# First stage of a hybrid attention / DeltaNet layer: a fixed table of single instructions in place of a list scheduler

## The chip, the cores and the metric

One core of one Trainium2 chip runs the kernel. The metric is the device time of one execution in microseconds, as the median of several runs. The profiled execution is a separate one, and its views give times within that execution's span.

## What is computed

One decoder layer over 512 tokens of width 1024, in fp32. The layer has two token mixers that read the same combined projection of x, a merge of the two, and an MLP:

```python
q, ck, cv, sk, sv, wk, wv, gates, qkv, beta, decay, gg, mg = split(x @ w_in)
o_nsa = g0 * compressed_attn + g1 * selected_block_attn + g2 * window_attn      # 8 heads of 64, 2 key groups
o_gdn = rms_norm(gated_deltanet(conv(qkv), beta, decay)) * silu(gg)              # 4 heads of 128, 4 chunks here
m = sigmoid(mg[:1024]) * (o_nsa @ w_nsa_out) + sigmoid(mg[1024:]) * (o_gdn @ w_gdn_out)
x = LN(alpha * x + m @ w_o)
x = LN(alpha * x + (silu(conv(x @ w_up)[gate]) * conv(x @ w_up)[val]) @ w_down)
```

## The kernel before

Every fp32 product is made of three f32r products of a high and a low half: `product` (L234) issues, for each of eight 128-row blocks, hi·hi (L239), hi·lo (L241) and lo·hi (L242), so that one weight unit of 128 output columns is 24 matmuls of 512 columns. `gemm_t` (L247) is such a unit: `split_w` (L215) loads 512 KB of weights into `raw` (DMA, L218), copies each half to f32r as `wh` (L225 on ACT, or L227 on DVE), subtracts for the rest `wl` (L229, DVE or POOL), and the product goes to a PSUM bank of the pool `pg` that has two.

The first stage (L261 to L882) begins with x: `load_x` (L209) loads and splits it, and `pb` products of 288 columns (L276 to L278) give the values and gate inputs token by token. Then come the small constants (L297 to L316), the decay terms `decays` (L331 to L367, whose prefix sums are the small matmuls L365), and steps named by a letter and a head. For GDN head h: `i` (`gdn_k`), `j` (`gdn_q`), `v` (`gdn_v`), `m` (`gdn_mid`: decay matrices and the kq products L482), `n` (`gdn_tri`: inverse of the triangular matrix, whose first block sums are L495, L497, L503 and the matmuls L505, and then 15 steps of two small DVE operations, L512 and L513), `o` (`gdn_out`: the four chunks in turn), `y` (`gdn_gate`: norm with the power L258 on POOL, transposes L397 of `y`, gating multiply L631 to `yT`). For attention: `k` keys, `q` queries of two heads, `c` the compressed blocks (L694 among others), `p` the compressed attention of a key group, `a` and `b` the six score units of a head, of which each goes through scores (L781, L782), a fused mask and maximum (L785), exp (L787), a scale (L798), transposes (L810), a split copy (L814, L815) and PV matmuls (L827, L832) into the one `pout` bank. `oT` (L838) takes a head's result. `g` is a merge product (`merge`, L855): a weight unit whose tanh goes to an SBUF tile `mt` (L858).

What sets the order before is a list scheduler. The step list `ORDER` (L128) gives each step a priority from its place, moved by `SHIFT` (L125); the weight splits are moved by `PRE` (L127); the scheduler then places the instructions of every engine one by one, taking what its own model holds ready by priority. Work tiles come out of pools with rotating buffers, a tag for each kind of use (`BUFS`, L129).

The merge stage follows (L884 to L928): `yoh` (copies L146 and L148 of `oT` and `yT`) and `yol` (L905), then for m from 0 to 7 a pair of `pm` products against `w_nsa_out` and `w_gdn_out`, each the size of half a unit, the gating, and the load and split of `w_o`. Five merge products are done in the first stage (`g0` to `g4`), two more ahead of m = 0, the rest between the pm products, in a PSUM pool `pg2` of their own:

```python
done = BUFS["mg"]
for m in range(8):
    while done < min(16, max(2 * m + 4, BUFS["mg"] + 2)):
        merge(done, mg2)
        done += 1
```

## Time and profile before

| | |
|---|---|
| time, 3 runs | median 842.46 us (842.21 to 843.61) |
| profiled execution | 845.36 us, of which span 843.6 us, mean granted clock 0.995 |
| TensorE busy | 822.8 us (98%) |
| VectorE, ScalarE, GpSimd busy | 637.8 (76%), 407.5 (48%), 145.4 us (17%) |
| chain that ended last | PE 80%, DVE 10%, ACT 3%, issue 3%, DMA 3% |
| first stage until the first pm matmul | 0 to 349.1 us |
| merge stage, output product, MLP | 349 to 843.6 us |

A matmul's recorded duration is longer than the distance to the next one, since they are pipelined. So a busy TensorE is not one at its rate: for the rate, the starts of successive matmuls are compared.

### The profile page before, as it was taken

Reading aid. Unit: us, or ns where it says so; the run is one execution under the profiler, and the core shown is the slowest. Engines: PE = TensorE matmul, PEld = TensorE weight load, DVE = VectorE, ACT = ScalarE, POOL = GpSimd, SP = SyncE. Lnnn points to the kernel's source line nnn. Section 1 sums busy time; section 2 is a strip of 40 time slices with the busy share of each in tenths; the row PEclk is TensorE's granted clock in tenths of the full one; section 3 lists DMA queues with packets and bytes.
Section 4 is the critical chain, followed back from the end, with each engine's and each line's share of the span. In section 5 each row is a group of like instructions: output and inputs, shape, how many; then the busy total and the mean of one; then the engine's idle time right before and its main releaser. Section 6 shows DMA issues by size and latency. Waiting matters only on the chain.

```text
span 843.6 us, 12073 instructions
## 1 busy us (share of the span) xinstructions
PE 822.8 (98%) x4226; PEld 679.7 (81%) x4226; DVE 637.8 (76%) x1373; ACT 407.5 (48%) x916; POOL 145.4 (17%) x127
## 2 busy tenths in 40 slices
PE   9899999999999999999999999999999999999996
PEld 8787787878777778888888898888888888788884
DVE  5856789987856985863457637888888988998578
ACT  5343577575457755442234114444444444566350
POOL 0131222313243321201400002101111111100001
PEclk9999999999999999999999999999999999999998
DMA  7323120002111101254346021555555566665762
GB/s 249 128 76 100 51 76 26 26 27 75 51 32 44 51 26 50 93 167 141 124 133 244 25 76 51 199 200 200 198 188 192 197 199 202 223 223 189 262 205 107
DMA packets 39820, 108.06 MB, mean 128 GB/s; under 512 B 4560, under 2 KB 4944, under 8 KB 39504
## 3 DMA queue, kind: packets, MB, share of 16 engines
q1 hardware_dynamic: 39760, 107.30, 38.5%
q8 instruction: 33, 0.54, 0.3%
q14 instruction: 27, 0.22, 0.1%
HBM read 93.65 MB, written 13.63 MB: 127 GB/s over the span
## 4 chain that ended last, share of the span: by engine, by line
PE 80%; DVE 10%; ACT 3%; issue 3%; DMA 3%; POOL 1%; SPq 0%; DVEq 0%; ACTq 0%; POOLq 0%
PE pu L241 9%; PE pu L239 9%; PE pu L242 9%; PE gps L241 7%; PE gps L239 7%; PE gps L242 7%; PE pout L827 2%; PE pw L988 2%; PE pw L989 2%; PE pw L990 2%; PE pm L242 2%; PE pm L239 2%; PE pm L241 2%; PE aps L810 2%; PE pdnb L1123 1%
## 5 line engine op out<-in xcount | busy, mean ns | idle before, releaser
L225 ACT ACTIVATE wh<-raw 128x512 fp32r<-128x512 f32 (+1 forms) x162 | 100.2, 621 | 122.7 <-PE pu L241 68.0
L239 PE MATMUL pu<-mh,wh 128*128 128x512 f32 (+1 forms) x384 | 142.7, 372 | 0.0
L241 PE MATMUL pu<-ml,wh 128*128 128x512 f32 (+1 forms) x384 | 142.6, 371 | 0.0
L242 PE MATMUL pu<-mh,wl 128*128 128x512 f32 (+1 forms) x384 | 142.6, 371 | 0.0
L229 DVE TENSOR_TENSOR wl<-raw,wh 128x512 fp32r<-128x512 f32 (+1 forms) x144 | 113.9, 793 | 34.7 <-ACT wh L225 33.2
L239 PE MATMUL gps<-xh,wh 128*128 128x512 f32 x320 | 128.5, 402 | 0.6 <-DVE kl L648 0.6
L241 PE MATMUL gps<-xl,wh 128*128 128x512 f32 x320 | 128.2, 401 | 0.0
L242 PE MATMUL gps<-xh,wl 128*128 128x512 f32 x320 | 127.8, 400 | 0.0
L239 PEld LDWEIGHTS pu<-mh,wh 128*128 128x128 f32 x384 | 72.3, 188 | 12.6
L242 PEld LDWEIGHTS pu<-mh,wl 128*128 128x128 f32 x384 | 72.3, 188 | 12.6
L241 PEld LDWEIGHTS pu<-ml,wh 128*128 128x128 f32 x384 | 72.3, 188 | 12.3
L229 POOL TENSOR_TENSOR wl<-raw,wh 128x512 fp32r<-128x512 f32 x40 | 53.7, 1343 | 153.0 <-ACT wh L225 81.0
L1067 DVE SCALAR_TENSOR_TENSOR fa<-pu,fcw,fa 128x511 f32<-128x511 f32 x88 | 65.7, 746 | 9.3 <-ACT fa L1064 7.9
L239 PEld LDWEIGHTS gps<-xh,wh 128*128 128x128 f32 x320 | 60.6, 189 | 11.6 <-issue 1.0
L242 PEld LDWEIGHTS gps<-xh,wl 128*128 128x128 f32 x320 | 60.7, 190 | 10.8
L241 PEld LDWEIGHTS gps<-xl,wh 128*128 128x128 f32 x320 | 60.7, 190 | 10.6
L1073 POOL TENSOR_TENSOR fth<-fth,fa 128x512 f32<-128x512 f32 x22 | 29.5, 1339 | 214.1 <-DVE fa L1067 199.9
L1114 DVE TENSOR_TENSOR dl<-raw,dh 128x512 fp32r<-128x512 f32 x69 | 46.0, 703 | 19.4 <-ACT dh L1113 19.2
L1113 ACT ACTIVATE dh<-raw 128x512 fp32r<-128x512 f32 x69 | 41.0, 626 | 36.5 <-DMA raw<-tdn 17.7
L787 ACT ACTIVATE sc<-sc,mn 128x384 f32<-128x384 f32 (+2 forms) x64 | 35.9, 562 | 16.2 <-DVE mn L785 11.7
L258 POOL TENSOR_TENSOR rs<-rs,minus_half 128x1 f32<-128x1 f32 x8 | 7.5, 941 | 163.3 <-DVE rs L949 163.3
L1064 ACT ACTIVATE fa<-pu,fcw 128x512 f32<-128x512 f32 x44 | 29.6, 672 | 10.2 <-PE pu L242 10.2
(350 smaller groups left out, 1688.8 us busy)
## 6 DMA issues: line engine op xcount, KB each, us to landing
raw<-in_up SPq DMA_DIRECT2D x44, 512.0 KB, 4.0
raw<-in_wT SPq DMA_DIRECT2D x40, 512.0 KB, 3.5
traw<-in_down SPq DMA_DIRECT2D x22, 512.0 KB, 4.8
tdn<-traw SPq DMA_DIRECT2D x44, 256.0 KB, 3.3
raw<-tdn SPq DMA_DIRECT2D x20, 512.0 KB, 4.4
raw<-in_down SPq DMA_DIRECT2D x15, 512.0 KB, 3.7
raw<-in_wm SPq DMA_DIRECT2D x8, 512.0 KB, 3.6
raw<-in_wo SPq DMA_DIRECT2D x8, 512.0 KB, 3.9
```

What stands on the lines that cost most here:

```text
L225: A.activation(wh, r, AF.Copy)
L229: eng.tensor_tensor(wl, r, wh.bitcast(F32), op=OP.subtract)
L239: i = PE.matmul(ps, wh[k], mh_(k), start=(k == 0), stop=False)
L241: PE.matmul(ps, wh[k], ml_(k), start=False, stop=False)
L242: PE.matmul(ps, wl[k], mh_(k), start=False, stop=(k == n - 1))
L787: A.activation(s[:, i, :n], s[:, i, :n], AF.Exp, scale=-1.0, bias=mn[:, 0, i:i + 1], accum_out=mn[:, 1, i:i + 1])
L810: PE.transpose(pt[:, i, k, :], s[:, i, k * 128:(k + 1) * 128], ident)
L1064: A.activation(acc, ps, AF.Copy, scale=w[:, 2:3])
L1067: V.scalar_tensor_tensor(acc[:, n:], ps[:, :S - n], w[:, i:i + 1], acc[:, n:], op0=OP.mult, op1=OP.add)
L1073: G.tensor_tensor(th, th, g[1], op=OP.mult)
L1113: A.activation(wh, raw[:, i], AF.Copy)
L1114: V.tensor_tensor(wl, raw[:, i], wh.bitcast(F32), op=OP.subtract)
```

## The change

Engine calls of the first stage are no longer issued where they are written. A `Queue` around each engine records them under the name of their step (`draw`), and a table `GIVEN` of 2,822 single instructions then gives them out one after the other, with no scheduler between (`tc.manual_schedule()`). An entry such as `q0P*12` stands for the next twelve TensorE instructions of step q0, `dV@2` for a certain one of the decays on DVE; weight units have steps of their own (`w20S`, `w20A`, `w20V`), so their load and split stand apart from the product; `s` and `f` with two digits are the score and the PV part of a unit. P has 1,610 entries, V 688, A 415, G 74, S 35. The instructions after the first stage are written and scheduled as before.

Work tiles of the stage come from `Places`: a fixed set of tiles of each size, of which a string names the one that each request gets. In place of ten tags there are ten sizes, shared between uses.

Seven merge products stand in the table. The sixth and seventh stay in the two `pg` banks, which are kept open past the stage, and `gate` (their tanh) is written behind the loop that makes `yoh` and `yol`. The merge stage asks for nine merge products ahead of m = 0, and takes its PSUM banks from the same `pg`.

```diff
-ORDER = "q0 k0 i0 q1 j0 m0 c n0 ...
-SHIFT = {'q0': -40, 'a0': -3470, ...
-PRE = {17: 2170, 13: -300, ...
+DRAWN = "q0 k0 i0 q1 j0 m0 c n0 ... g3 a7 g4 b7 y3 g5 g6".split()
+GIVEN = """
+w20S w20A w20V w20A w20V n0V@2 q0P*12 w18S dV@2 dV@3 dA@1 w0S q0P*10 dV@4 dV@5 dV@6 w18A n2G@1 w18A w18V dV@7 w18V
...
+y3V y3P*4 y3V f75A f75V g6P
+""".split()
+    class Queue:
+        def __getattr__(self, name):
+            give = getattr(self.engine, name)
+            def note(*a, **kw):
+                if not into:
+                    return give(*a, **kw)
+                steps[into[-1]].setdefault(self.letter, []).append((give, a, kw))
+            return note
...
+    class Places:
+        def tile(self, shape=(128, S), dt=F32):
+            t = self.all[next(self.turn)][:shape[0], :math.prod(shape[1:])]
...
-        acc = slot("in", "acc")
+        acc = R["big"].tile()
...
     def merge(i, pl):
-        ps = gemm_t(24 + i)
+        MG[i] = gemm_t(24 + i)
+        if pl is not None:
+            gate(i, pl)
+
+    def gate(i, pl):
         t = pl.tile([128, S], F32, name="mt", bufs=BUFS["mg" if pl is mgp else "mr"])
-        A.activation(t, ps, AF.Tanh, scale=0.5)
+        A.activation(t, MG[i], AF.Tanh, scale=0.5)
         MG[i] = t
...
-    for step in ORDER:
-        with tc.high_priority(offset=-(at + SHIFT.get(step, 0))):
-            f(*[int(step[1:])] if step[1:] else [])
...
+    with tc.manual_schedule():
+        for step in GIVEN:
+            name, at, k = step.partition("@")
+            name, _, n = name.partition("*")
+            for _ in range(int(n or 1)):
+                part = todo[name]
+                i = int(k) if at else next(i for i, x in enumerate(part) if x)
+                give, a, kw = part[i]
+                part[i] = None
+                give(*a, **kw)
...
     pm = ps2.enter_context(tc.tile_pool(name="pm", bufs=2, space=PSUM))
-    pg = ps2.enter_context(tc.tile_pool(name="pg2", bufs=2, space=PSUM))
-    gps = lambda shape=(128, 512): pg.tile(list(shape), F32, name="gps")
...
     done = BUFS["mg"]
+    while done in MG:
+        gate(done, mg2)
+        done += 1
     for m in range(8):
-        while done < min(16, max(2 * m + 4, BUFS["mg"] + 2)):
+        while done < min(16, max(2 * m + 4, BUFS["mg"] + 4)):
             merge(done, mg2)
             done += 1
```

Three places of the two orders follow. In the names of the changed kernel `pg_171` and `pg_172` are the two banks of `pg`, `po_398` is the `pout` bank, `pd` and `pa` are other PSUM tiles, and `big` and `row` are work tiles; L252 and L1023 are the lines from which all its recorded or given calls are issued.

SyncE's queue at the start, before (from the last but one block of `wB` on):

```order
8 L218 DMA raw<-in_wB 128x576
9 L218 DMA raw<-in_wT 128x1024
10 L211 DMA xr<-in_xT 128x512
11 L297 DMA cst<-in_consts 128x1444
12 L300 DMA ident<-in_consts 128x128
13 L307 DMA gcw<-in_gcw 128x48
14 L309 DMA fcw<-in_fcw 128x132
```

And now (from the last block of `wB` on):

```order
11 L252 DMA raw_156<-in_wB 128x576
12 L252 DMA big_94<-in_xT 128x512
13 L252 DMA cst<-in_consts 128x1444
14 L252 DMA ident<-in_consts 128x128
15 L252 DMA gcw<-in_gcw 128x48
16 L252 DMA fcw<-in_fcw 128x132
17 L252 DMA gnw<-in_gnw 128x1
18 L252 DMA alog<-in_glog 128x4
19 L252 DMA gdt<-in_gdt 128x4
20 L1023 DMA raw_157<-in_wT 128x1024
```

The first weight unit (`in_wT`) stood ahead of the last load of x; now it stands behind it and behind the seven loads of constants.

TensorE at the first block sums of GDN head 0, before: the last two kq products (L482), what lies between, and the block sums (L505):

```order
290 L482 MATMUL dps<-kq 128x256
291 L694 MATMUL aps<-kv,raw 128x155 x3
292 L241 MATMUL gps<-xl,wh 128x512
293 L242 MATMUL gps<-xh,wl 128x512
294 L239 MATMUL gps<-xh,wh 128x512
295 L241 MATMUL gps<-xl,wh 128x512
296 L242 MATMUL gps<-xh,wl 128x512
297 L239 MATMUL gps<-xh,wh 128x512
298 L241 MATMUL gps<-xl,wh 128x512
299 L242 MATMUL gps<-xh,wl 128x512
300 L505 MATMUL dps<-gx,cst 128x512
```

And now (`pd_394<-kq` is the last kq product, `pd_393<-big_87,cst` the first block sum):

```order
260 L1023 MATMUL pg_171<-xl,wh_160 128x512
261 L1023 MATMUL pd_394<-kq_117 128x256
262 L1023 MATMUL pg_172<-xh,wh_161 128x512
263 L1023 MATMUL pg_172<-xl,wh_161 128x512
...
278 L1023 MATMUL pg_172<-xh,wl_162 128x512
279 L1023 MATMUL pg_172<-xh,wh_159 128x512
280 L1023 MATMUL pg_172<-xl,wh_159 128x512
281 L1023 MATMUL pg_172<-xh,wl_162 128x512
282 L1023 MATMUL pg_172<-xh,wh_159 128x512
283 L1023 MATMUL pd_393<-big_87,cst 128x512
```

Between the last kq product and the first block sum there were three matmuls of 155 columns and eight of 512; there are now 21 of 512 (rows 262 to 282).

ACT at the end of the first stage, before:

```order
374 L146 ACTIVATE ob<-pout 64x512
375 L611 ACTIVATE gt<-gps 128x512
376 L146 ACTIVATE yoh<-oT 128x512 x2
377 L146 ACTIVATE yoh<-yT 128x512 x4
378 L858 ACTIVATE mt<-gps 128x512
```

And now:

```order
386 L252 ACTIVATE wh_159<-raw_157 128x512
387 L1023 ACTIVATE big_109<-po_398 64x512
388 L252 ACTIVATE yoh<-oT 128x512 x2
389 L252 ACTIVATE yoh<-yT 128x512 x4
390 L252 ACTIVATE mt<-pg_172 128x512
391 L252 ACTIVATE mt<-pg_171 128x512
```

TensorE there, now (`pd_393<-ident,big_101` are the transposes of `y` of GDN head 3; `pg_171` and `pg_172` are the banks in which the seventh and the sixth merge product lie):

```order
1423 L1023 MATMUL po_398<-pc_154,vcb 128x512
1424 L1023 MATMUL po_398<-pc_155,vcb 128x512
1425 L1023 MATMUL pd_393<-ident,big_101 128x128 x4
1426 L1023 MATMUL pg_171<-xh,wl_164 128x512
1427 L252 MATMUL pg_172<-xh,wh_161 128x512
1428 L252 MATMUL pg_172<-xl,wh_161 128x512
```

The tanh that reads a merge product stood behind the six `yoh` copies before and stands behind them now. Before, TensorE wrote the next product into another bank than the one which that tanh reads; now the next one (row 1427) goes into `pg_172`, which the first of the two tanh reads.

## Rows read from the trace of the kernel before

**Rows 1.** The page's first, second and sixth section: busy time of the engines in the whole span, the granted clock in 40 equal slices, and the loads of the weight units (KB each, median us from issue to landing).

```profile
PE 822.8 (98%) x4226; PEld 679.7 (81%) x4226; DVE 637.8 (76%) x1373; ACT 407.5 (48%) x916; POOL 145.4 (17%) x127
...
PEclk9999999999999999999999999999999999999998
...
raw<-in_wT SPq DMA_DIRECT2D x40, 512.0 KB, 3.5
```

**Rows 2.** Busy time of each engine in stretches of the program (length, then PE, PEld, DVE, ACT, POOL busy with the count of instructions, granted clock, DMA share, GB/s): one stretch inside the first stage, the last two merge products, and the merge stage from its first pm matmul on.

```profile
140.00:180.00 40.00, 38.16 (x247) 30.21 (x245) 36.73 (x116) 23.70 (x58) 11.87 (x10) 1.00 0.14 41
341.00:349.00 8.00, 8.00 (x37) 6.61 (x36) 5.93 (x11) 5.71 (x10) 2.92 (x2) 1.00 0.21 68
349.00:442.00 93.00, 93.00 (x412) 77.02 (x411) 51.02 (x66) 31.23 (x48) 18.84 (x15) 1.00 0.43 142
```

**Rows 3.** TensorE's instructions between the first matmul of q0 and the first pm matmul, grouped by line, operands and shape (count; busy, mean ns; idle time in front of them): the six costliest of 45 groups.

```profile
L239 PE MATMUL gps<-xh,wh 128*128 128x512 f32 x248 | 100.5, 405 | 0.6 <-DVE kl L648 0.6
L241 PE MATMUL gps<-xl,wh 128*128 128x512 f32 x248 | 100.2, 404 | 0.0
L242 PE MATMUL gps<-xh,wl 128*128 128x512 f32 x248 | 99.8, 403 | 0.0
L810 PE MATMUL aps<-ident,sc 128*128 128x128 f32 x160 | 28.1, 276 | 1.1 <-DVE sc L798 1.0
L827 PE MATMUL pout<-pth,vcat 128*128 128x256 f32 x96 | 26.9, 304 | 1.1 <-DVE oT L838 1.0
L827 PE MATMUL pout<-ptl,vcat 128*128 128x256 f32 x96 | 25.0, 291 | 0.2 <-DVE ptl L815 0.2
...
```

**Rows 4.** TensorE's timeline at three places (start, duration, line, operands, count): a PV matmul of 256 columns and the one five starts later; four transposes and the matmul behind them; and two pm matmuls of 512 columns, six starts apart. The distance from start to start is the rate.

```profile
335.64 0.27 PE L827 MATMUL pout<-pth,vcat 128*128 128x256 f32 x1
...
336.23 0.28 PE L827 MATMUL pout<-ptl,vcat 128*128 128x256 f32 x1
...
339.99 0.66 PE L397 MATMUL dps<-ident,y 128*128 128x128 f32 x4
340.40 0.47 PE L241 MATMUL gps<-xl,wh 128*128 128x512 f32 x1
...
349.13 0.39 PE L239 MATMUL pm<-yoh,wh 128*128 128x512 f32 x1
...
350.49 0.39 PE L239 MATMUL pm<-yoh,wh 128*128 128x512 f32 x1
```

**Rows 5.** TensorE's waits in the first stage, by what was waited for (total us, times, longest): the two largest of 13 entries, and the smallest.

```profile
PE dps L365 <- issue: 1.7, 1, 1.7
PE dps L505 <- DVE gx L503: 1.6, 2, 1.2
...
PE pout L827 <- DVE ptl L815: 0.2, 1, 0.2
```

**Rows 6.** SyncE's timeline in the start: the first weight unit's load, the last load of x, the last small load, and the second weight unit's load.

```profile
11.13 0.33 SPq L218 DMA_DIRECT2D raw<-in_wT  x1
11.51 0.42 SPq L211 DMA_DIRECT2D xr<-in_xT  x1
...
16.33 0.33 SPq L316 DMA_DIRECT2D gdt<-in_gdt  x1
17.18 0.33 SPq L218 DMA_DIRECT2D raw<-in_wT  x1
```

**Rows 7.** The load issued at 17.18 us (KB, us from issue to landing).

```profile
raw<-in_wT SPq DMA_DIRECT2D x1, 512.0 KB, 4.6
```

**Rows 8.** TensorE's timeline at the start of q0: the first product matmul.

```profile
19.98 0.39 PE L239 MATMUL gps<-xh,wh 128*128 128x512 f32 x1
```

**Rows 9.** TensorE's timeline around the decay matmuls (L365): they themselves with the idle time in front, and the first and last of nine products that start from 32.20 to 35.55 us.

```profile
30.51 0.81 PE L365 MATMUL dps<-gdec,cst 128*128 128x16 f32 x6 [1.73 <-issue]
...
32.20 0.57 PE L239 MATMUL gps<-xh,wh 128*128 128x512 f32 x1
...
35.55 0.45 PE L242 MATMUL gps<-xh,wl 128*128 128x512 f32 x1
```

**Rows 10.** Busy time and granted clock (the column behind POOL) just after that wait, and after a wait of 1.18 us elsewhere.

```profile
33.00:35.00 2.00, 2.00 (x6) 1.63 (x5) 0.06 (x1) 0.44 (x1) 0.85 (x1) 0.50 0.44 88
76.00:80.00 4.00, 4.00 (x16) 2.48 (x15) 3.59 (x15) 1.89 (x7) 0.07 (x1) 1.00 0.43 114
```

**Rows 11.** Timeline of all engines around the first block sum of GDN head 0 (L505): the last of the matmuls behind which its chain begins, the first operation of the chain (on POOL), and the block sum behind it.

```profile
71.32 0.59 PE L482 MATMUL dps<-kq 128*128 128x256 f32 x2
...
72.51 1.30 POOL L495 TENSOR_TENSOR lo<-m,cst 128x512 f32<-128x512 f32 x1 [9.54 <-issue]
...
75.74 1.53 PE L505 MATMUL dps<-gx,cst 128*128 128x512 f32 x4 [1.18 <-DVE gx L503]
```

**Rows 12.** Timeline at the end of the first stage: the gating multiply L631, DVE's last half-head add L838, ACT's yoh copies, and the tanh of the sixth merge product.

```profile
337.93 0.69 DVE L838 TENSOR_TENSOR oT<-pout,ob 64x512 f32<-64x512 f32 x1
...
340.69 0.75 DVE L631 SCALAR_TENSOR_TENSOR yT<-dps,gnw,gs 128x512 f32<-128x512 f32 x1 [0.15 <-PE dps L397]
...
341.55 1.16 ACT L146 ACTIVATE yoh<-oT 128x512 fp32r<-128x512 f32 x2 [3.25 <-DVE yT L631]
...
342.61 2.18 ACT L146 ACTIVATE yoh<-yT 128x512 fp32r<-128x512 f32 x4
...
344.70 0.58 ACT L858 ACTIVATE mt<-gps 128x512 f32<-128x512 f32 x1
```

More of the change, by code (lines that the diff above doesn't have):

```diff
@@ L134, in body, with __init__, draw @@
     nc = tc.nc
-    V, A, G, PE = nc.vector, nc.scalar, nc.gpsimd, nc.tensor
+    steps, into = {}, []
+    class Queue:
+        def __init__(self, engine, letter):
+            self.engine, self.letter = engine, letter
+        def __getattr__(self, name):
[5 more added lines that the diff above has]
+            return note
+    V, A, G, PE, SP = (Queue(*e) for e in zip((nc.vector, nc.scalar, nc.gpsimd, nc.tensor, nc.sync), "VAGPS"))
+    def draw(name, f, *at):
+        steps[name] = {}
+        into.append(name)
+        f(*at)
+        into.pop()
     def E(name, h, d="V"):
@@ L178, in fill, with __init__ @@
                 self.small.tile([128, left // 4], F32, name="rest")
+    class Places:
+        def __init__(self, make, name, n, size):
+            self.all = [make([128, size], F32, name=f"{name}{i}", bufs=1) for i in range(n)]
+            turn = [int(c, 36) for c in PLACE.get(name, "")]
+            again = turn[-n:] if len(set(turn[-n:])) == n else range(n)
+            self.turn = itertools.chain(turn, itertools.cycle(again))
+        def tile(self, shape=(128, S), dt=F32):
+            t = self.all[next(self.turn)][:shape[0], :math.prod(shape[1:])]
+            if dt is not F32:
+                t = t.bitcast(dt)
+            if len(shape) > 2:
+                names = "abcd"[:len(shape) - 1]
+                t = t.rearrange(f"p ({' '.join(names)}) -> p {' '.join(names)}", **dict(zip(names, shape[1:])))
+            return t
     psum = lambda name, bufs: ctx.enter_context(tc.tile_pool(name=name, bufs=bufs, space=PSUM))
@@ L209, in load_x @@
     def load_x(k):
-        xr = slot("mid", "xr")
-        nc.sync.dma_start(out=xr, in_=d["xT"][:, k, :])
+        xr = R["big"].tile()
+        SP.dma_start(out=xr, in_=d["xT"][:, k, :])
         A.activation(xh[:, k, :], xr, AF.Copy)
@@ L222, in split_w @@
             r = raw[:, i * half:(i + 1) * half]
-            wh = wp.tile([128, half] + list(shape[2:]), F32R, name="wh", bufs=BUFS["wh"])
+            wh = R["wh"].tile([128, half] + list(shape[2:]), F32R)
             if first is A:
@@ L227, in split_w @@
                 first.tensor_copy(wh, r)
-            wl = wp.tile([128, half] + list(shape[2:]), F32R, name="wl", bufs=BUFS["wl"])
+            wl = R["wl"].tile([128, half] + list(shape[2:]), F32R)
             eng.tensor_tensor(wl, r, wh.bitcast(F32), op=OP.subtract)
@@ L236, in product, with split, gemm_t @@
         (wh, wl), (mh_, ml_) = w, m
-        first = None
         for k in range(n):
-            i = PE.matmul(ps, wh[k], mh_(k), start=(k == 0), stop=False)
-            first = first or i
+            PE.matmul(ps, wh[k], mh_(k), start=(k == 0), stop=False)
             PE.matmul(ps, wh[k], ml_(k), start=False, stop=False)
             PE.matmul(ps, wl[k], mh_(k), start=False, stop=(k == n - 1))
-        return first
-    HOLD = {}
-    def gemm_t(u, eng=None, after=None):
-        with tc.high_priority(offset=PRE.get(u, 0)):
-            w = split_w(d["wT"][u], [128, KD, 128], E("ws", u, "G"), E("wh", u, "A"))
+    W = {}
+    def split(u):
+        W[u] = split_w(d["wT"][u], [128, KD, 128], E("ws", u, "G"), E("wh", u, "A"))
+    def gemm_t(u):
+        if into:
+            draw(f"w{u}", split, u)
+        else:
+            split(u)
         ps = gps()
-        first = product(ps, w, (lambda k: xh[:, k, :], lambda k: xl[:, k, :]), KD)
-        if after is not None:
-            tc.add_manual_dep(first.ins, after.ins.name, mybir.DependencyInfo(
-                mybir.DependencyClass.NoSync, mybir.DependencyReason.SCHED_ONLY), reason="its rows have no room before")
+        product(ps, W.pop(u), (lambda k: xh[:, k, :], lambda k: xl[:, k, :]), KD)
         return ps
@@ L426, in gdn_k @@
         rn = norms(h, 0, pk)
-        gk = st["gk"] = sp.tile([128, 4, TT], F32, name="gk", bufs=2)
+        gk = st["gk"] = R["row"].tile((128, 4, TT))
         V.tensor_tensor(gk[:, 0], rn, rn, op=OP.mult)
@@ L625, in gdn_gate @@
         V.tensor_tensor(t, t, cq, op=OP.mult)
-        y = slot("out", "y", c4)
+        y = R["big"].tile(c4)
         rowscale(E("y", h), y, ot, so[:, 2, :, None])
@@ L636, in keys @@
     def keys(g):
-        ps = gemm_t(18 + g, after=HOLD.get("k") if g else None)
-        hh_ = nsa.tile([128, 2, S], F32R, name="kh")
-        ll_ = nsa.tile([128, 2, S], F32R, name="kl")
+        ps = gemm_t(18 + g)
+        hh_ = R["k"].tile((128, 2, S), F32R)
+        ll_ = R["k"].tile((128, 2, S), F32R)
         KK[g] = (hh_, ll_)
@@ L652, in queries @@
     def queries(pr):
-        ps = gemm_t(20 + pr, after=HOLD.get(2 * pr - 3))
-        qf = slot("qf", "qf")
+        ps = gemm_t(20 + pr)
+        qf = R["big"].tile()
         for i in range(2):
@@ L670, in compressed @@
     def compressed():
-        cst_ = ExitStack()
-        ct = pool(cst_, name="ct", bufs=1, side="left")
-        kv = ct.tile([128, 5, 8, 32], F32, name="kv")
+        kv = ctp.tile([128, 5, 8, 32], F32, name="kv")
         w2 = nsa.tile([128, 128], F32, name="w2")
-        nc.sync.dma_start(out=w2, in_=d["w2"])
+        SP.dma_start(out=w2, in_=d["w2"])
         pos = nsa.tile([128, 2, 16], F32, name="pos")
-        nc.sync.dma_start(out=pos, in_=d["pos"])
+        SP.dma_start(out=pos, in_=d["pos"])
         V.memset(kv[:, 4], 0.0)
@@ L818, in flip @@
         if u == 1:
[L819 removed]
+            POUT[h] = R["po"].tile()
         pout = POUT[h]
```

317 lines of the change are left out of this document (207 added, 110 removed).

## The prediction

> **What bounds the kernel now.** I read the page first, then stretches of the program, then TensorE's instructions and waits in the first stage, and at last the timelines at the places where the change moves something. By the page TensorE is busy for 98% of the span, and its clock is at the full level in nearly every slice [rows 1]. The stretches show where that share comes from. From the first pm matmul on, TensorE is busy without a break, 93.0 of 93.0 us in the merge stage, while DVE has 51 us of work there and ACT 31 [rows 2]. Behind 349 us it is TensorE's rate that sets the time, so what the first stage gains comes through to the end, and what it loses too.
>
> A busy TensorE is not one at its rate. A matmul of 512 columns is recorded with 0.39 us, but the next one starts 0.227 us later (six starts in 1.36 us) [rows 4]. A gap of up to 0.16 us between two such matmuls therefore shows as busy. So I priced the first stage from start to start. From the first q0 matmul at 19.98 us [rows 8] to the first pm matmul at 349.13 us [rows 4] it is 329.2 us. In it there are 744 product matmuls at 0.227 us (168.7 us), 192 PV matmuls of 256 columns at 0.118 (22.7), and 160 transposes at 0.103 (16.4) [rows 3, 4]; the 39 smaller groups of that view, each by its own distance, come to about 88 us. The sum is 296 us: **about 33 us of the first stage are lost** in waits and slow stretches. The list of waits names only 9.8 us in 13 entries, from 1.7 down to 0.2 us [rows 5]; the rest lies in gaps under a long record, and in product matmuls that follow each other at 0.23 us and more.
>
> The Trainium skill, in Perfetto Trace Analysis, section Identifying the Most-Contended Engine, says that the busy share of matmuls is no good measure of the room that is left, because pipelined instructions look smaller in a trace. Taken as a measure, the busy share would leave 843.6 - 822.8 = 20.8 us in the whole kernel; by starts there are 33 in the first stage alone.
>
> **What the change does, part by part.** It neither adds nor removes arithmetic, and TensorE has the same matmuls. What differs is the order, hence the 33 us, and three places.
>
> *Start.* SyncE now issues the first weight unit behind the last load of x and seven loads of constants. Before, it was issued at 11.13 us and the last of those loads at 16.33 [rows 6]. In its new place it goes out at about 16.2 us. A load issued at 17.18 us took 4.6 us [rows 7], and the median of these loads is 3.5 [rows 1]; the copy to f32r, of the tanh's size, is another 0.6 [rows 12]. So q0 starts at 20.3 to 21.4 us, against 19.98 [rows 8]. I take +0.9 us, with ends of 0 (the last load of x, now first in line, brings the pb products forward) and +2.
>
> *Decays.* TensorE waited 1.73 us for the decay matmuls, behind only 32 product matmuls, and a little later nine products started over 3.35 us, from 32.20 to 35.55, where eight steps at full rate are 1.81 [rows 9]: the granted clock stood at 0.50 there, the 1.2 GHz level [rows 10]. Now these matmuls stand behind three whole products or nearly so, some 15 us after the start of q0, where the wait before ended 10.5 us after it. Both go: **-1.7 us and -1.5 us**.
>
> *Inside the stage.* Of the 33 us these leave 29.8. The first block sum shows how they arise and what the table does about them. The chain from the last kq matmuls (71.32 us) through POOL and DVE to the block sum (75.74) takes about 4.0 us counted from the end of those matmuls, and TensorE had 2.6 us of work for it and then waited 1.18 [rows 11]. In the new order 21 matmuls of 512 columns lie there, 21 x 0.227 = 4.8 us; the same place in the other three heads holds 5 us or more. Elsewhere the table sets single matmuls between the links of a chain in the same way, mostly with as much as the link needs and little over. The bounds: 3 us stay at least, if every link is covered (744 matmuls at 0.004 us over the rate); 29.8 stay at most if nothing is, and more only by the rival below. I followed some 35 places where cover and chain are within 0.3 us of each other; if each costs the smallest named wait, 0.2 us [rows 5], that is 7 us. With the 3 and another 1 for longer misses I take 11 us, nearer to the covered end because the place in the rows is covered with room to spare. **-18.8 us**.
>
> *End of the stage.* Here the change adds a wait. The two last products now lie in the only two `pg` banks, and the next product goes to the bank that ACT's first tanh reads, behind six yoh copies. By the rows of before: transposes of y start at 339.99, one product matmul later TensorE would be free at 340.63 [rows 4]; the gating multiply ends at 341.44, the half-head add (0.69 us), which now stands behind it, at 342.1; ACT's six copies take 3.24 us (341.55 to 344.79), the tanh 0.58 [rows 12]. With 0.1 us for each hand-over the tanh ends at 346.1. TensorE stands for **5.5 us**, where before it ran on without a gap, since its next product had another bank [rows 2]. Nothing else is queued on TensorE that could go first. Behind it, the yol subtractions and weight splits have 10.9 us of products as cover. Two products move from the merge stage, which has 93 us of TensorE work and 51 of DVE [rows 2], into the time before it; it then has 82 against 51 and stays with TensorE, so the move itself costs nothing. Ends: 0 if the copies could run before the add, 6.5 if the add comes late.
>
> *Clock.* The wait of 1.73 us was followed by the half clock, one of 1.18 us was not [rows 9, 10]. After 5.5 us I expect it, at the same price as before: **+1.5 us**, with ends of 0 and 3.1 (a second such stretch at the start, where TensorE now stands about 3 us before q0).
>
> *Work tiles.* Shared fixed places can make an instruction wait for a tile's last reader where the old pools had another buffer. That is part of the 11 us above; the weight loads are issued early enough in the table that a load of 3.5 us [rows 1] is covered.
>
> Sum: 0.9 - 1.7 - 1.5 - 18.8 + 5.5 + 1.5 = **-14.1 us**. All terms come from the profiled execution (845.36 us with a span of 843.6); the median of the runs is 2.9 us lower, and I apply the sum to that: 842.46 - 14.1 = **828.4 us**.
>
> **Rivals.**
> 1. *Only named waits can go.* If the rest of the 33 us belongs to the matmuls themselves (they start at 0.23 us and more wherever another engine reads the same memory), the table can win 9.8 us of waits and 1.5 of clock: -11.3 + 0.9 + 5.5 + 1.5 = -3.4, or 839 us. For it: the page's 98%. Against it: in the merge stage the same matmuls keep 0.227 us beside a DVE that is at work for half of the time [rows 2, 4].
> 2. *The wait at the end doesn't come, or costs little.* Then -14.1 + 7.0 = -21.1, or 821 us. Against it: the order itself, in which the copies stand ahead of the tanh.
> 3. *Slower: a fixed order has no give.* An instruction of the table that comes late holds up everything behind it on its engine. The place is DVE, which gets runs of up to 13 small operations of one chain in a row, and which in a stretch such as 140 to 180 us is already busy for 36.7 of 40 us [rows 2]: a wl subtraction or a scale behind such a run comes late and TensorE stands for it. If the inner loss then stays where it was, the sum is 0.9 - 3.2 + 7.0 = +4.7, or 847 us. It decides at an inner loss of 25.1 us; below that the kernel is faster. Against it: a late instruction leaves the others where they are, and the cover at the block sums has grown.
>
> **How the numbers follow.** The forecast with its bounds (inner loss 5 to 18 us) has 0.60, rival 1 0.13, rival 2 0.12, rival 3 0.12, and 0.03 is left for a result within 0.2%, about 1.7 us, which a measurement of this kernel can't tell from no change. The first three lie on the faster side; a little of rival 1 reaches into the middle. That gives faster 0.83, same 0.05, slower 0.12. The range: at the low end an inner loss of 5 us and no clock loss, -14.1 - 6 - 1.5 = -21.6, or rival 2, some 819; at the high end the loss of rival 1 and 2 us on top, 841. Outside stay rival 3 and the tails.
>
> **What would show it.** In the changed kernel's trace: the first q0 matmul at 20.3 to 21.4 us; no wait ahead of the decay matmuls, and no clock of 0.50 in the following 5 us; no wait of over 0.3 us at the block sums; a wait of TensorE of 5 to 6 us behind the transposes of y of head 3, ended by a tanh, and perhaps the half clock behind it; some 82 us from the first pm matmul to the end of the merge stage; and the first pm matmul at about 329.2 - 14.1 + 10.9 = 326 us after that of q0. The forecast is wrong if the waits inside the stage add up to far more than 11 us, or if the merge stage shows waits of TensorE where two products fewer lie.

## The result, and the profile after

The changed kernel takes **832.26 us** (median of 4 runs, 831.48 to 835.69) against 842.58 us for the kernel before on the same chip: ratio 0.9883, with a 95% interval of 0.9855 to 0.9912. That is 10.3 us less, where 14.1 were forecast. A second set of runs gave 0.9876 (0.9862 to 0.9889).

The profiled execution after has a span of 833.9 us, 9.7 less than before. It is the longest of the four (835.69 us), 3.4 us above their median, as the profiled execution before lies 2.9 us above its own; the second set's trace (e9, span 830.7) is used beside it. The page of the kernel after, busy times and granted clock, which answer to [rows 1]:

```profile
PE 813.7 (98%) x4226; PEld 685.5 (82%) x4226; DVE 636.8 (76%) x1373; ACT 403.8 (48%) x916; POOL 143.5 (17%) x127
...
PEclk9999999999999999899999999999999999999999
```

TensorE's share is 98% as before, and its busy time is 9.1 us less with the same matmuls: much of what went was hidden under long records, as [rows 3, 4] had it. The clock line dips in one slice; the windows below show the stretches.

TensorE's waits after, from q0 to the end, by what was waited for (total us, times, longest). They answer to [rows 5]:

```profile
PE pg L252 <- ACT mt L252: 5.3, 1, 5.3
PE pg L1023 <- ACT wh L1023: 1.8, 1, 1.8
PE pdna L252 <- DVE dl L252: 1.5, 1, 1.5
PE pw L252 <- DVE mt L252: 0.8, 1, 0.8
PE pt L252 <- DVE x L252: 0.4, 1, 0.4
PE po L1023 <- DVE ptl L1023: 0.4, 1, 0.4
```

In place of the 13 named waits inside the first stage (9.8 us) there is one of 0.4 us, at a PV matmul. But two are new at the stage's edges (the tanh 5.3, the first weight split 1.8), and three lie behind the stage.

The end of the first stage after, all engines, which answers to [rows 12]: the transposes of y (PE), the last matmul of the seventh product, DVE's gating multiply and half-head add, ACT's yoh copies and tanh, and the next product.

```profile
327.58 0.66 PE L1023 MATMUL pd<-ident,big 128*128 128x128 f32 x4
...
327.99 0.47 PE L1023 MATMUL pg<-xh,wl 128*128 128x512 f32 x1
...
328.27 0.75 DVE L1023 SCALAR_TENSOR_TENSOR yT<-pd,gnw,big 128x512 f32<-128x512 f32 x1 [0.75 <-PE pd L1023]
...
329.06 0.68 DVE L1023 TENSOR_TENSOR oT<-po,big 64x512 f32<-64x512 f32 x1
...
329.86 1.15 ACT L252 ACTIVATE yoh<-oT 128x512 fp32r<-128x512 f32 x2 [1.73 <-DVE oT L1023]
...
330.91 2.17 ACT L252 ACTIVATE yoh<-yT 128x512 fp32r<-128x512 f32 x4
...
333.11 1.09 ACT L252 ACTIVATE mt<-pg 128x512 f32<-128x512 f32 x2
...
333.76 0.79 PE L252 MATMUL pg<-xh,wh 128*128 128x512 f32 x1 [5.30 <-ACT mt L252]
...
339.47 0.43 PE L252 MATMUL pg<-xl,wh 128*128 128x512 f32 x1
```

The chain is the one that the order showed: the add behind the gating multiply, six copies behind the add, the tanh behind the copies, the product behind the tanh. TensorE stands for 5.30 us, and then the clock is at its lower level: 13 steps take from 333.76 to 339.47, 0.44 us each.

The start after (TensorE: last pb matmul, first q0 matmuls, and a slow stretch that follows), which answers to [rows 8]:

```profile
18.82 0.29 PE L252 MATMUL pb<-wh,xl 128*128 128x288 f32 x1
20.89 0.50 PE L1023 MATMUL pg<-xh,wh 128*128 128x512 f32 x1 [1.79 <-ACT wh L1023]
...
22.26 0.63 PE L1023 MATMUL pg<-xl,wh 128*128 128x512 f32 x1
...
25.61 0.40 PE L1023 MATMUL pg<-xh,wh 128*128 128x512 f32 x1
```

q0 starts at 20.89 us, 0.91 us later than before. From 22.26 to 25.61 a step is 0.42 us, eight in all. The load that q0 waits for, its place on SyncE's queue (three merged) and its size and time to landing, which answer to [rows 6, 7]:

```profile
13.39 2.55 SPq L1023 DMA_DIRECT2D raw<-in_wT  x3
...
raw<-in_wT SPq DMA_DIRECT2D x1, 512.0 KB, 6.7
```

It goes out at 13.39 us and lands 6.7 us later.

The granted clock (the column behind POOL's busy time) in that stretch and behind the tanh; the last row is the merge stage up to the first output matmul and answers to [rows 2]:

```profile
23.00:25.00 2.00, 2.00 (x6) 1.54 (x6) 1.26 (x5) 0.46 (x1) 0.00 (x0) 0.50 0.86 231
...
334.00:339.00 5.00, 5.00 (x12) 3.89 (x13) 2.52 (x3) 1.28 (x3) 3.25 (x3) 0.50 0.01 3
347.50:430.03 82.53, 81.75 (x361) 67.37 (x359) 43.76 (x60) 28.63 (x44) 14.69 (x12) 1.00 0.42 140
```

Put end to end, in the two profiled executions: q0 starts 0.91 us later; from there to the first pm matmul it is 326.60 us instead of 329.15, with 10.9 us of products more in it, so 13.4 us less for the same work; from there to the first output matmul 82.54 instead of 92.48 - 10.9 = 81.6, so 0.9 us more; from there to the end of the last matmul 395.7 instead of 394.0, so 1.7 more; and 0.2 behind it. The sum is -9.7.

### The profile page after: what moved, and what is told of

It is laid out like the page before. It is cut to its first block, busy times and chain, and to the rows that moved or that the text cites. A ratio compares the mean times of both kernels' runs of the same rounds, so it can differ in the third digit from the quotient of the medians.

```text
span 833.9 us, 12016 instructions
## 1 busy us (share of the span) xinstructions
PE 813.7 (98%) x4226; PEld 685.5 (82%) x4226; DVE 636.8 (76%) x1373; ACT 403.8 (48%) x916; POOL 143.5 (17%) x127
## 4 chain that ended last, share of the span: by engine, by line
PE 86%; DVE 6%; DMA 4%; ACT 2%; issue 2%; POOL 0%; SPq 0%; DVEq 0%; ACTq 0%; POOLq 0%
PE pu L252 27%; PE pg L1023 20%; PE pd L1023 7%; PE pg L252 6%; PE pa L1023 5%; PE pm L252 5%; PE pdna L252 5%; PE pdnb L252 4%; PE pw L252 3%; PE po L1023 3%; DMA raw<-in_down 2%; DVE x L252 1%; DVE wl L252 1%; DMA raw<-in_wT 1%; DMA big<-in_xT 1%
## 5 line engine op out<-in xcount | busy, mean ns | idle before, releaser
L252 PE MATMUL pu<-mh,wh 128*128 128x512 f32 (+1 forms) x384 | 142.7, 372 | 0.0
L252 PE MATMUL pu<-ml,wh 128*128 128x512 f32 (+1 forms) x384 | 142.6, 371 | 0.0
L252 PE MATMUL pu<-mh,wl 128*128 128x512 f32 (+1 forms) x384 | 142.6, 371 | 0.0
L252 ACT ACTIVATE wh<-raw 128x512 fp32r<-128x512 f32 (+2 forms) x120 | 75.5, 632 | 110.7 <-PE pu L252 70.0
L252 DVE TENSOR_TENSOR wl<-raw,wh 128x512 fp32r<-128x512 f32 (+2 forms) x116 | 93.7, 810 | 37.2 <-ACT wh L252 37.0
L1023 PE MATMUL pg<-xh,wh 128*128 128x512 f32 x248 | 100.2, 407 | 1.8 <-ACT wh L1023 1.8
L1023 PE MATMUL pg<-xl,wh 128*128 128x512 f32 x248 | 99.2, 401 | 0.0
L1023 PE MATMUL pg<-xh,wl 128*128 128x512 f32 x248 | 97.7, 399 | 0.0
L252 PEld LDWEIGHTS pu<-ml,wh 128*128 128x128 f32 x384 | 72.3, 188 | 12.6
L252 PEld LDWEIGHTS pu<-mh,wh 128*128 128x128 f32 x384 | 72.3, 188 | 12.6
L252 PEld LDWEIGHTS pu<-mh,wl 128*128 128x128 f32 x384 | 72.3, 188 | 12.3
L252 DVE SCALAR_TENSOR_TENSOR fa<-pu,fcw,fa 128x511 f32<-128x511 f32 x88 | 65.7, 746 | 9.3 <-ACT fa L252 7.9
L252 POOL TENSOR_TENSOR fth<-fth,fa 128x512 f32<-128x512 f32 x22 | 29.5, 1340 | 214.1 <-DVE fa L252 199.9
L252 DVE TENSOR_TENSOR dl<-raw,dh 128x512 fp32r<-128x512 f32 x69 | 46.6, 705 | 18.4 <-ACT dh L252 18.2
L252 ACT ACTIVATE dh<-raw 128x512 fp32r<-128x512 f32 x69 | 41.7, 627 | 35.4 <-DVE dl L252 10.4
L1023 PEld LDWEIGHTS pg<-xh,wh 128*128 128x128 f32 x248 | 47.1, 190 | 10.7 <-ACT wh L1023 2.0
L1023 ACT ACTIVATE big<-big,mn 128x384 f32<-128x384 f32 (+3 forms) x84 | 45.6, 554 | 21.1 <-DVE mn L1023 20.3
L1023 PEld LDWEIGHTS pg<-xh,wl 128*128 128x128 f32 x248 | 46.9, 190 | 8.9 <-DVE wl L1023 0.4
L1023 PEld LDWEIGHTS pg<-xl,wh 128*128 128x128 f32 x248 | 47.0, 189 | 8.3
L1023 POOL TENSOR_TENSOR wl<-raw,wh 128x512 fp32r<-128x512 f32 x28 | 36.3, 1306 | 80.6 <-ACT wh L1023 49.7
L252 POOL TENSOR_TENSOR rs<-rs,minus_half 128x1 f32<-128x1 f32 x8 | 7.5, 942 | 166.1 <-DVE rs L252 166.1
L252 PE MATMUL pg<-xh,wh 128*128 128x512 f32 x72 | 29.4, 408 | 5.3 <-ACT mt L252 5.3
```

The lines of the kernel that those rows point to most:

```text
L252: return give(*a, **kw)
L1023: give(*a, **kw)
```

## The experiments

The theory after the result: the table covers the chains inside the stage; the two products moved into it lose part of that again by the bank that they share, and the start and the PSUM layout lose a little more. The rival: what the stage gains and loses is one sum, set by the chains and by DVE, and an edge that is mended comes back as another wait.

| run | edit | us, median | ratio to before (95%) |
|---|---|---|---|
| the change | | 832.26 | 0.9883 (0.9855 to 0.9912) |
| e9_change_again | none | 832.64 | 0.9876 (0.9862 to 0.9889) |
| e1_gates_first | both tanh ahead of the copies | 828.29 | 0.9824 (0.9807 to 0.9841) |
| e2_tanh_in_stage | sixth tanh in the table | 825.62 | 0.9792 (0.9777 to 0.9806) |
| e3_early_load | first weight load ahead of the last x | 830.2 | 0.9848 (0.9834 to 0.9863) |
| e4_less_cover | 11 matmuls behind the block sum | 834.6 | 0.9897 (0.988 to 0.9913) |
| e5_five_in_table | products six and seven out of the table | 827.53 | 0.981 (0.979 to 0.9829) |
| e6_before_decays_late | kernel before, decay matmuls later | 845.85 | 1.0027 (1.0015 to 1.0039) |
| e7_before_seven | kernel before, seven products in the stage | 844.72 | 1.0015 (1.0006 to 1.0025) |
| e8_pw_bank | other bank for the first output product | 831.42 | 0.9856 (0.9838 to 0.9874) |
| e10_three_mended | e2, e3 and e8 together | 823.24 | 0.9759 (0.9746 to 0.9773) |
| e11_five_mended | e5, e3 and e8 together | 823.95 | 0.9769 (0.9755 to 0.9782) |

Between chips the kernel before itself moves from 842.6 to 843.6 us, so the ratios are compared; 0.001 is 0.84 us.

**The wait behind the copies.** Two runs take it away in different ways.

```diff
+    done = BUFS["mg"]
+    while done in MG:
+        gate(done, mg2)
+        done += 1
     yol = []
...
-    done = BUFS["mg"]
-    while done in MG:
-        gate(done, mg2)
-        done += 1
```

> The two tanh of the sixth and seventh product are written ahead of the yoh copies. Their tiles lie where the first stage's tiles were, so the first can begin only when the last half-head add is done (329.75 in the trace after). Theory that the tanh behind the copies makes the wait of 5.3 us: the tanh begins at about 329.9 instead of 333.1, the wait is 2.1 us, the half clock behind it (about 2.8 us lost) goes or shrinks; 826 to 829 us against 832.3. Rival, that the copies themselves are late and pm then waits for yoh and yol: the wait only moves, 831 to 833 us.

The end of the stage in e1 (both tanh on ACT, and the product behind them):

```profile
328.35 1.09 ACT L252 ACTIVATE mt<-pg 128x512 f32<-128x512 f32 x2 [1.73 <-DVE oT L1023]
...
328.99 0.67 PE L252 MATMUL pg<-xh,wh 128*128 128x512 f32 x1 [2.04 <-ACT mt L252]
```

The wait is 2.04 us, as the theory had it, and the ratio falls by 0.0059, 5.0 us, against the change's first set and by 0.0052 (4.4) against its second; 3.3 of it are wait. The half clock still comes, for nine steps (328.99 to 332.75, 1.7 us over the full rate). It was 13 steps in the trace after but nine in e9's too, so the runs don't show that the shorter wait made it shorter.

```diff
-BUFS = {... 'mg': 5, ...
+BUFS = {... 'mg': 6, ...
-y3A*2 f71P g6P*2 ...
+y3A*2 g5A f71P g6P*2 ...
-        while done < min(16, max(2 * m + 4, BUFS["mg"] + 4)):
+        while done < min(16, max(2 * m + 4, BUFS["mg"] + 3)):
```

> The sixth product gets a tile in the first stage's own pool, and its tanh is given in the table behind its product; the seventh stays in its bank as before. The next product then finds its bank free. Theory that the shared bank costs a wait and a clock stretch, 5.3 + 2.8 us: TensorE goes on without a gap for 5.4 us, after which the next weight split, which ACT makes behind the copies, may cost 1 to 2 us; no half clock: 824 to 828 us. Rival, that the chain behind the stage's end sets the time and the wait was hidden room: 830 us or more, with waits of the same sum a little later.

The same place in e2 (the sixth product's tanh; the last matmul of the table and the first of the next product; the seventh product's tanh):

```profile
317.46 0.60 ACT L1023 ACTIVATE mt<-pg 128x512 f32<-128x512 f32 x1
...
326.92 0.40 PE L252 MATMUL pg<-xh,wl 128*128 128x512 f32 x1
...
327.16 0.39 PE L252 MATMUL pg<-xh,wh 128*128 128x512 f32 x1
...
331.28 0.60 ACT L252 ACTIVATE mt<-pg 128x512 f32<-128x512 f32 x1
```

The sixth tanh is done 9 us ahead, TensorE steps on after 0.24 us, and the trace has no wait at all until pm, and no half clock there. From the first q0 matmul to the first pm matmul it takes 316.79 us instead of 326.60. The ratio falls by 0.0091, 7.7 us (0.0084, 7.1, against the second set), of 5.3 + 2.8 that the profile had put down to the place. The rival falls: behind the wait only a pm matmul was late, by 0.3 us.

**The start.**

```diff
             hi, lo = split_w(d["wB"][:, k0:k0 + 2, :], [128, 2, 288], V)
+            if k0 == KD - 2:
+                draw("w20", split, 20)
+                give, a, kw = steps["w20"]["S"].pop(0)
+                give(*a, **kw)
             load_x(k0 + 1)
...
-        if into:
+        if u == 20:
+            pass
+        elif into:
             draw(f"w{u}", split, u)
...
-w20S w20A w20V ...
+w20A w20V ...
```

> The load of the first weight unit is issued ahead of the last load of x, as before the change; all else is as in the change. Theory that the start costs 0.9 us of later q0 and 1.7 us of half clock behind the idle time ahead of it: q0 at 20.0 us, no half clock from 22 us on, 829.5 to 830.5 us. Rival, that the pb products are held up by as much and the clock falls anyway: 831.5 to 833.

The first q0 matmul in e3, without a wait ahead of it:

```profile
19.08 0.40 PE L1029 MATMUL pg<-xh,wh 128*128 128x512 f32 x1
```

It starts 1.8 us sooner than in the trace after, and 0.9 sooner than before the change, since the pb products end sooner too. No half clock follows. The ratio falls by 0.0035 (2.9 us) against the change's first set, by 0.0028 (2.4) against its second: the theory's size, though both intervals overlap e3's. Its parts are not the theory's. In e9's trace q0 starts at 20.58 us and no half clock follows, so most of what the early load is worth there is the 1.5 us by which q0 is sooner.

**Cover.** The block sum of head 0 after, which answers to [rows 11] (last kq product; the chain's last operation, on DVE; the block sum):

```profile
60.30 0.59 PE L1023 MATMUL pd<-kq 128*128 128x256 f32 x2
...
63.83 0.69 DVE L1023 TENSOR_TENSOR big<-ts,cst 128x512 f32<-128x512 f32 x1
...
65.53 1.02 PE L1023 MATMUL pd<-big,cst 128*128 128x512 f32 x2
```

From the recorded end of the kq product (60.89) the chain takes 3.6 us, to the end of the DVE operation at 64.52. TensorE, with its 21 matmuls, comes to the block sum only at 65.53, and there is no wait. The counter-test takes eleven of them away from there:

```diff
-... cA cP*11 cA*2 m0V@4 n0G m0V*2 ...
+... cA cA*2 m0V@4 n0G m0V*2 ...
-... n0G n0P s03P ...
+... n0G n0P cP*11 s03P ...
```

> Eleven product matmuls are given behind the first block sum of head 0 instead of ahead of it, so that 10 stand between the last kq product and the block sum, not 21; nothing else moves. Theory that the inner gain is cover of chains: chain 4.0 us, cover 10 x 0.227 = 2.3, a wait of 1.7 us at the block sum (none now), 833.5 to 834.5 us. Rival, that TensorE's own rate and not the order sets the stage: no wait over 0.5 us and 832 to 832.6.

The last kq product and the block sum in e4:

```profile
58.40 0.59 PE L1023 MATMUL pd<-kq 128*128 128x256 f32 x2
...
62.65 1.12 PE L1023 MATMUL pd<-big,cst 128*128 128x512 f32 x2 [1.35 <-DVE big L1023]
```

A wait of 1.35 us appears, 0.35 less than reckoned: from the recorded end of the kq product (58.99) to the block sum it is 3.7 us here, not 4.0, of which the ten matmuls cover 2.3. The ratio goes up by 0.0014 (1.2 us) against the first set of the change, 0.0021 (1.8) against the second. The intervals overlap, so the time alone settles little; the wait in the trace does. It isn't given back: from q0 to pm e4 takes 326.67 us where e9 takes 324.04, with no half clock at the start in either; 1.0 of the 2.6 is a longer half clock behind the tanh (14 steps instead of nine), and 1.6 are left.

**Five or seven.** In e5 all entries of g5, g6 and their weight units w29 and w30 leave the table. By the loop's new bound two products, not the four of the expectation, then run ahead of m = 0, as in the kernel before; from q0 to the first pm matmul the trace has 745 records of product matmuls, the kernel before 744.

```diff
-DRAWN = "... b7 y3 g5 g6".split()
+DRAWN = "... b7 y3".split()
...
-        while done < min(16, max(2 * m + 4, BUFS["mg"] + 4)):
+        while done < min(16, max(2 * m + 4, BUFS["mg"] + 2)):
```

> The table without its sixth and seventh product (48 matmuls and their loads and splits): five merge products in the first stage, the next four ahead of m = 0, in the two banks that are free by then. Theory that the two products are cover at the end of the stage and cost a wait behind it: up to 10.9 us of TensorE work go from between the last chains, which then show as waits of 5 to 10 us; the wait of 5.3 us and its clock stretch (2.8) go: 828 to 836 us, a near draw. Rival, that seven products instead of five is where the gain comes from: 838 or more. Rival, that it costs only: 824.

TensorE's largest waits at the end of the stage and behind it, up to the output product, in e5:

```profile
PE pd L1021 <- DVE big L1021: 0.8, 1, 0.8
PE pw L250 <- DVE mt L250: 0.8, 1, 0.8
PE pm L250 <- POOL yol L250: 0.8, 1, 0.8
```

The theory of cover fails here in its size: with 48 matmuls gone from the last steps, the largest wait that appears is 0.8 us, not 5 to 10. Gaps under long records don't show either: from q0 to pm e5 takes 306.80 us and e2, with the two products and no tanh wait, 316.79, so that the products' 10.9 us cost 10.0 there. What covers the last chains instead was not tried. So the two products in the table are worth about 1 us there, and with their wait they cost 0.0073, 6.2 us (5.6 against the second set). The other way round, in the kernel before:

```diff
-ORDER = "... g4 b7 y3".split()
+ORDER = "... g4 b7 y3 g5 g6".split()
-BUFS = {... 'mg': 5, ...
+BUFS = {... 'mg': 7, ...
```

> The kernel before, with the sixth and seventh merge product as steps of its first stage and seven tiles for them, so that the scheduler may place them there. Theory that the number of products in the stage is not the gain, since before the change they already ran without a gap behind the transposes of head 3: 840 to 844 us. Rival, that they fill gaps of the stage under the scheduler too: 830 to 837.

Under the list scheduler seven products give 1.0015, a little slower. The number of products is not where the gain comes from.

**The decays alone.**

```diff
-        for i, n in enumerate(("upper", "after", "ones")):
-            PE.matmul(ps[:, i * 16:(i + 1) * 16], C[n], gv, start=True, stop=True)
+        with tc.high_priority(offset=-1000):
+            for i, n in enumerate(("upper", "after", "ones")):
+                PE.matmul(ps[:, i * 16:(i + 1) * 16], C[n], gv, start=True, stop=True)
```

> The kernel before, with the three decay matmuls at a lower priority: they come 34 TensorE rows later. Theory that they cost 1.7 us of wait and 1.5 us of half clock behind it: no wait at them, 838.5 to 840 us against 842.5. Rival, that the half clock comes by itself or the wait turns up elsewhere: 841 to 843.

TensorE in e6 at three places of the start, with what it waited for:

```profile
32.54 0.47 PE L239 MATMUL gps<-xh,wh 128*128 128x512 f32 x1 [1.17 <-DVE qf L150]
...
38.10 0.74 PE L366 MATMUL dps<-gdec,cst 128*128 128x16 f32 x6
...
41.24 0.47 PE L239 MATMUL gps<-xh,wh 128*128 128x512 f32 x1 [2.40 <-DVE kl L649]
```

This expectation was wrong: the rival in it, that the wait turns up elsewhere, came true, and the time is 0.27% longer. The decay matmuls no longer wait (38.10), but TensorE now stands 1.17 us for a query eviction (DVE's copy of a finished query product out of its PSUM bank) and 2.40 us for the split of the keys (L648 before, L649 here), which was 0.6 us in the kernel before [rows 3]; behind the 2.40 us the half clock comes.

Where the wait of 1.73 us in [rows 9] came from can be seen beside e7's trace, in which DVE runs the same instructions in the same order from its first copy of the constants up to the split of the keys. That copy and TensorE's product behind the key split, in the kernel before; then in e7 the same two, with the decay matmuls between:

```profile
20.03 0.29 DVE L508 COPY xs<-cst 128x64 f32<-128x64 f32 x2 [0.93 <-DMA cst<-in_consts]
...
41.37 0.47 PE L239 MATMUL gps<-xh,wh 128*128 128x512 f32 x1 [0.59 <-DVE kl L648]
...
18.94 0.29 DVE L508 COPY xs<-cst 128x64 f32<-128x64 f32 x2
...
29.39 0.81 PE L365 MATMUL dps<-gdec,cst 128*128 128x16 f32 x6 [0.69 <-issue]
...
38.83 0.47 PE L239 MATMUL gps<-xh,wh 128*128 128x512 f32 x1 [0.81 <-DVE kl L648]
```

In the profiled execution before, DVE stood for the load of the constants, and its decay chain began 1.1 us later than in e7. In e7 the decay matmuls wait 0.69 us, the granted clock behind them is 1.00 (windows from 28 to 44 us), and with the same 72 product matmuls since q0 the product behind the key split starts 2.5 us sooner. So a good part of the loss at the decays seems to belong to an execution in which the constants came late; this compares two executions, and no edit tests it. That the table's order on DVE, where the decays' operations stand one by one between those of q0 and k0, wins something in this stretch was not tried by itself.

**A bank of the output product.** Behind the merge stage, the last pm matmul, DVE's gating and the first output matmul after:

```profile
428.86 0.39 PE L252 MATMUL pm<-yoh,wl 128*128 128x512 f32 x1
...
429.29 0.69 DVE L252 SCALAR_TENSOR_TENSOR mt<-mt,pm 128x512 f32<-128x512 f32 x1 [2.03 <-PE pm L252]
...
430.03 0.50 PE L252 MATMUL pw<-woh,mh 128*128 128x512 f32 x1 [0.78 <-DVE mt L252]
```

```diff
+    pt3 = ps3.enter_context(tc.tile_pool(name="pt3", bufs=2, space=PSUM))
     pw = ps3.enter_context(tc.tile_pool(name="pw", bufs=1, space=PSUM))
-    pt3 = ps3.enter_context(tc.tile_pool(name="pt3", bufs=2, space=PSUM))
```

> The change, with the PSUM pools of the output product opened in the other order, so that its first product lies in another bank than the last pm product. Theory that the first output matmul's wait of 0.78 us for DVE comes from the shared bank (the pg banks are kept in place, which moves pm): no wait there, 831 to 831.7 us against 832.3. Rival, that the wait moves to another operand: 832 to 832.6.

The same place in e8:

```profile
426.15 0.39 PE L252 MATMUL pm<-yoh,wl 128*128 128x512 f32 x1
426.37 0.39 PE L252 MATMUL pw<-woh,mh 128*128 128x512 f32 x1
```

The wait is gone; the step is 0.22 us. From the first pm matmul to the first output matmul it takes 81.60 us, 0.94 less than in the trace after. This is what the theory asks for: keeping `pg` open moved the pm tiles to other banks, and the pools opened after them took over the bank that DVE still read; no view shows the bank numbers themselves. The ratio is 0.0027 lower than the first set and 0.002 than the second, 1.7 to 2.3 us, more than the 0.9 of the place; both intervals overlap, so the rest isn't shown.

**Together.**

> The change itself, on the same chip as the next two, to set the scale: ratio to before 0.988, with its times 2 to 4 us apart by how much of the stretch behind the wait of 5.3 us runs at the half clock.

TensorE in e9 at the two edges of the stage: the first q0 matmul, the product behind the tanh, and the first matmul at full rate behind that:

```profile
20.58 0.50 PE L1023 MATMUL pg<-xh,wh 128*128 128x512 f32 x1 [1.35 <-ACT wh L1023]
...
331.86 0.79 PE L252 MATMUL pg<-xh,wh 128*128 128x512 f32 x1 [5.29 <-ACT mt L252]
...
335.76 0.39 PE L252 MATMUL pg<-xh,wh 128*128 128x512 f32 x1
```

The wait behind the copies is the same as in the trace after, but nine steps run at the lower clock and not 13, and none at the start. The four times lie 2.7 us apart.

> The change with three edits at once: the sixth product's tanh in the stage, the first weight load ahead of the last load of x, and the output product's other banks. Theory that the losses are separate and add: against the change -6.6 -2.1 -0.8 = -9.5 us, ratio to before 0.977. Rival, that the early start only lengthens a later wait: 0.979 or more.

> Five merge products in the table, with the early load and the other banks. Theory that the sixth and seventh product give nothing as cover inside the stage, so that all of the gain is the order: -4.7 -2.1 -0.8 against the change, ratio 0.978 to 0.979, level with the kernel beside it. Rival, that two more products in the stage are worth something once their wait is gone: 0.981 or more, 2 us behind the other.

TensorE's two largest waits from 10 us to the end in e10:

```profile
PE pdna L252 <- DVE dl L252: 0.8, 1, 0.8
PE po L1029 <- DVE ptl L1029: 0.4, 1, 0.4
...
```

On one chip: 0.9876 for the change, 0.9759 with the three edits, 0.9769 with five products. The three edits add within what the intervals can tell: 9.9 us between the first two, where each by itself against the same set of the change gave 7.1, 2.4 and 1.7. From q0 on, nothing in the first stage waits for over 0.4 us, so the rival, by which a mended edge comes back as another wait, is out. With its wait gone, the pair of products in the table makes no difference that these intervals can tell (0.0010). e10, at 823.24 us, beats both kernels.

## Why the prediction was right, and where its terms were off

- **TensorE's rate bounds everything behind 349 us, and about 33 us are lost before.** Right. The named waits were 9.8 us, and the stage gave back more than that. Rival 1, by which only named waits can go, is out.
- **Inside the stage, -18.8 us.** From q0 to the first pm matmul 13.4 us went. Taking out the parts that are seen by themselves, 5.3 us of tanh wait, 2.8 of clock behind it (5.71 us less 13 steps of 0.227), 1.5 of clock at the start (eight steps in 3.35 us) and the 3.2 forecast for the decays, leaves 13.4 + 5.3 + 2.8 + 1.5 - 3.2 = 19.8 us. The trace of e10, where tanh wait and slow stretches are gone, gives the same without this bookkeeping: 316.81 us from q0 to pm, less 10.9, is 23.2 less than before, or 20.0 beside the 3.2. The size is right. That it is cover is shown at one place by e4; how it divides over the other places was not tried. Nor was the count of 35 places at 0.2 us each that made up most of the 11 us left: no view shows it, so that part of the agreement may be luck. At the place that the term argues from, its own parts, 2.6 of work and 1.18 of wait, give a chain of 3.8 us and not 4.0. The table also came with shared work tiles, and no run tries the one without the other.
- **Decays, -1.7 and -1.5.** Both are gone in the trace after, but the working was wrong: it took the wait for the price of three matmuls' place. e6 moved the matmuls, and other waits came in its stead. By the comparison with e7's trace, 1.0 of the 1.7 and the whole half clock go with the late constants of the profiled execution. The half clock is not in most executions either: seven runs of the kernel before beside e1 have a mean granted clock of 0.997 or 0.998, the profiled one 0.995. By an estimate, 0.997 leaves at most 5.9 us at the lower level in the whole span; every trace here has at least 2.8 us of that at the program's end alone, so that the 3.4 us behind the decays find no room. The sum, with this 1.5 in it, was applied to the median.
- **Start, +0.9.** Measured 0.91, by luck: the load goes out at 13.39 us and not at about 16.2, and takes 6.7 us and not 3.5 to 4.6. The two errors cancel. That a stretch at half clock would follow stood only as an end of the clock's term.
- **End of the stage, +5.5.** Measured 5.30, by the chain that the rows gave. Rival 2 is out.
- **Clock, +1.5. This term was mis-sized**: it took one stretch of the length seen before, and in the profiled execution there were two, of 2.8 and 1.5 us. Of the 4.4 us by which the sum was too good against the profiled spans, 2.8 are here. It isn't the same from run to run: behind a wait of 5.29 or 5.30 us the slow stretch cost 1.4 us in e3, 1.9 in e9, 2.7 in e8, 2.8 after and 2.9 in e4, and of these five only the trace after has the one at the start.
- **The move of two products costs nothing.** Wrong by 0.9 us: the move itself is free, but the bank layout that came with it is not (e8). The output product and the MLP took 1.7 us more, of which 1.2 is a wait at the first down products (1.5 us instead of 0.3). With a second wait just behind it this is 1.1 to 1.8 us in every kernel with the table. In the trace after, ACT's copy of the down weights ahead of it waits 2.27 us for a load of 512 KB that takes 5.5 us, where before it waited 0.28 us for one of 3.5. Why the load takes longer stays open.
- **The first pm matmul 326 us behind that of q0.** Measured 326.60, and 324.04 in e9. But the 0.9 of the start lies ahead of q0 and doesn't belong in that sum, which without it is 325.1.
- **Rival 3, a fixed order has no give.** Out: a single named wait of 0.4 us is left inside the stage, with DVE as loaded as before (636.8 us busy instead of 637.8).
- The sum of the prediction's terms with their measured sizes: 0.9 - 3.2 - 19.8 + 5.3 + 4.3 + 0.9 + 1.7 + 0.2 = -9.7 us, the difference of the profiled spans. The inner term is what the others leave, so it carries their errors, and the sum must come out; the others are read from the traces. For the medians, which the forecast was about, e9 and e7 have nearer sizes. An estimate with 0.6 for the start, -0.7 for the decays, 1.9 for the clock and 1.6 for the MLP is 0.6 - 0.7 - 19.8 + 5.3 + 1.9 + 0.9 + 1.6 = -10.2 us, beside 10.3 measured. In it the decays are 2.5 us less than forecast, bank and MLP another 2.5, and the inner term gives 1.0 back.

## What to carry to other kernels

Price a stretch of back-to-back matmuls from start to start: here half of what an exact order gave back lay under records that read as busy. When a step moves ahead of a stage's end, follow the buffer that its result stays in up to its reader's place on that engine's queue; two products moved for cover cost 5.3 us and a slow clock because one tanh stood behind six copies, and one more tile undid it. A wait names what came last there, not what would mend it: moving the three waiting matmuls only moved the wait. And before a term read from one profiled execution is put into a forecast of the median, look whether that execution is like the median: here its lower clock was not.

## What the runs showed that was not expected

The same wait had different prices: behind 5.29 or 5.30 us of it, seven (e3), nine (e9), 13 (after, e8) or 14 matmul steps (e4) ran at the lower clock. Which waits were followed by it at all: 1.73 us (before), 1.79 (after), 2.04 (e1), 2.40 (e6) and those of 5.3; not 1.51 at the down products (after), 1.35 at the start (e9) and at the block sum (e4), or the shorter ones in [rows 10] and in e6. In the trace after the clock had already fallen, in the windows from 332.5 us on, when TensorE began again at 333.76. And a pool of PSUM banks that is closed later moved the pools opened after it: 0.78 us at the first output matmul.
